# A hybrid token mixer with a routed MoE on one core: issue points of front work moved

## The chip, the cores and the metric

The kernel runs on one core of one Trainium2 chip. The metric is device microseconds of the whole program; lower is better. The times before are the median of three runs.

## The reference

One layer, 1024 tokens of width 1024, all in float32.

1. A conditioning vector gives six rows (shift, scale and gate, two times): `mod = silu(c) @ w_mod + b_mod`, six blocks of 1024.
2. `h = rms_norm(x) * (1 + sc1) + sh1`, then one projection to 2576 columns, split into three mixers: gated linear attention (GLA: q, k, v, output gate, and a low-rank decay gate), RetNet retention (q, k with rotation, v, gate), and an S5 state-space layer (16 groups of 16 channels with a complex state of 64, a scan over time, GELU and a GLU).
3. Attention layers work in chunks of 64 tokens: scores inside a chunk, a state from chunk to chunk; each head's output is normalised and multiplied by its gate. The three results are concatenated and sent through an output projection: `x = x + g1 * mixed @ w_out`.
4. `h2 = rms_norm(x) * (1 + sc2) + sh2`; a router picks 4 of 32 experts for each token; each expert is an up projection, a clamped SwiGLU and a down projection; the gated sum is added, then a final norm.

## The kernel before

Each float32 weight is used as two f16 parts (high and low); a product is three matmuls. `split` makes the parts: the high part on ACT (L182), the low part on DVE (L183). A projection of one tile (`proj_group`, lines 729 to 733) is 24 matmuls of 128 x 384, with a call `mid()` in the middle at which other work is issued.

The 1024 tokens are eight tiles of 128. The front (up to 578 us) has three stages, and the MoE follows. In the front the order in the program is the order of each engine's queue: an engine takes its instructions one after the other, and an instruction that waits holds up all behind it on its engine. PSUM tiles come in four tags: `j` (2 banks), `g` (3), `s` (2), `o` (1).

**First pass (to about 105 us).** The modulation rows, the norm of each tile (`n1_sum`, `n1_norm`, `n1_turn`, `n1_scale`), `n1_split` (the transposed tile as high and low f16; the low part by a subtraction at L673 on POOL, or on DVE), then `n1_proj`: S5's input and the decay gate (L187 belongs to it, through `mm3`). Behind the last tile come the first tile's projections q/k, g and v, with steps of `prep` in between.

**GLA loop (L1230 and on, to about 324 us).** Round h has `gla_decay(h)` (exponentials on ACT, L1070 to L1072), `gla_qk(h)` (projection and five DVE products), `gla_scores(h - 1)`, `gla_gate(h)`, `gla_out(h - 1)`, `gla_turn(h)`, `gla_v(h)` and `gla_norm(h - 1)`. In between, `filler(n)` takes the next n steps of a generator: S5 first, then the second weight set. S5 has four rounds b of `s5_products` (INJ on DVE at L900 to L902; its transposes to injT, L907; GE on POOL, L911 to L913; KS, L919; eight DMAs; cosine and sine tables) and `s5_scan` (L936, L942 with L945 and L946, the scan, L957, L967 and L970), then `s5_gate` with the GELU and four GLU pieces (L1013 to L1022). `weights2` splits the retention weights (`split_next`, which also issues the next weight load) and computes modulation blocks 2 and 3.

**Third pass (L1549 and on, to 578 us).** Round i starts with three loads on SP (`load_res(i)`: the tile's x, tile `x3` with two buffers; `load_hT(i + 2)`; `load_rope(i + 2)`), then `ret_qk(i + 1)` with the rotation on DVE, `ret_scores(i)`, `out_a(i - 1)` (output projection, first part), `out_turn(i - 2, 0)`, `ret_out(i)` (state, attention, head statistics), `ret_gate(i + 1)`, `out_turn(i - 2, 1)` (copy on DVE, L617), `ret_norm(i)`, `out_b(i - 1)`, `out_route(i - 2)` (router, top 4; L186 to L188 and L1475 on), `ret_v(i + 1)`, `out_place(i - 2)` (places in the expert lists, L1501, and four scatter DMAs on POOL), `ret_turn(i + 1)` (four transposes, L1323), `ret_end(i)` (transposes of the head output, L864), `out_rms(i - 1)` and `out_norm(i - 1)` (the norm of the next layer: L1445 on DVE, L1446 and L1449 on POOL). The old x tile is the scratch of that norm, so its buffer comes free when the subtraction at L1449 is done. The calls `f()` take steps of `weights3`:

```python
for k in OUT_ORDER: split_next(wO...); yield        # eight splits
split(rw16...); yield
for ac in mod_block(4): yield                       # row load, then 8 products L378
...; for sl, p in mod_rows(ac): ... a2 ...; yield   # L385 on PE, L1530 on DVE
ready.add("a2")
for ac in mod_block(5): yield                       # the same for block 5
... g2c (L1538 on PE)
```

`mod_block(b)` clears `ac` on POOL (L374), loads the bias row on SP (L375), and yields; then each step is one DVE product (L378) and one more weight load (`load_next`, L223). `ac` has one buffer. `out_norm(0)` reads a2, so a loop takes steps until `"a2"` is in `ready`.

**MoE (L1722 and on).** Blocks of rows are gathered by the id table that the scatters of `out_place` wrote, and run through the experts; weights stream in by SP.

Of the kernel before, what the change touches and what calls it, by code (L numbers as in the profile page):

```python
# [11 lines left out]
F32 = mybir.dt.float32  # L12
# [9 lines left out]
NT = T // 128  # L22
# [6 lines left out]
C_GQ, C_GK, C_GV, C_GG, C_GA = 0, 192, 384, 768, 1152  # L29
# [94 lines left out]
def build(ctx, tc, A, out, dbg=None):  # L124
# [269 lines left out]
    LR, LI = UC, US  # L394
# [271 lines left out]
    def n1_split(i, eng=G, parts=1):  # L666
        if i < NT:
            hd = hds.pop(i)
            hT = ht1[i] = p1.tile([128, 2, 8, 128], F16, name="hTa", bufs=3)
            for q in range(parts):  # L670
                ks = slice(q * 8 // parts, (q + 1) * 8 // parts)
                S.copy(hT[:, 0, ks], hd[:, ks])
                eng.tensor_tensor(hT[:, 1, ks], hd[:, ks], hT[:, 0, ks], op=SUB)  # L673
# [103 lines left out]
    rest = load_rest()  # L777
    for i in range(NT):
        def ahead():
            n1_split(i + 1)  # L780
            n1_norm(i + 2)
            if i == 0:
                n1_sum(3)

        n1_proj(i, ahead)
        n1_decay(i - 1)
        n1_turn(i + 2)
        n1_scale(i + 2)
        n1_store(i + 1)
        if i in (0, 1, 2):  # L790
            load_next()
        fill(rest)
        if i in (3, 4):
            load_hT(i - 3)
        if i == 5:
            s5_turned()
        if i == 6:
            s5_bias()
        fill(prep, 4)
        split_next(wA[:, 0, i, :], wA[:, 1, i, :], GLA_COLS)  # L800
        n1_sum(i + 4)
# [2 lines left out]
    gpj = {"qk": proj_group(hTs[0], wA, C_GQ, C_GV, mid)}  # L804
    mid()
    gpj["g"] = proj_group(hTs[0], wA, C_GG, C_GA, mid)
    mid()
    gpj["v"] = proj_group(hTs[0], wA, C_GV, C_GG, mid, "s")
    for _ in prep:
        pass  # L810
    dump("suT", suT.rearrange("p m l n -> p (m l n)"))
# [75 lines left out]
    def s5_products(b, B):  # L887
        gs = slice(4 * b, 4 * b + 4)
        GE = B["GE"] = s5w.tile([128, 4, 9, SH], F32, name="GE")
        tg = s5w.tile([128, 4, 8, SH], F32, name="tg", bufs=1)  # L890
        INJ = s5w.tile([128, 4, SL, SH], F32, name="INJ", bufs=1)

        def ch(x, q, n):
            return x[:, 4 * b + q, None, :].to_broadcast([128, n, SH])

        def pw(x, q, n):
            return x[:, 4 * b + q, 0:n, None].to_broadcast([128, n, SH])

        for q in range(4):
            V.tensor_tensor(INJ[:, q], ch(bb, q, 8), pw(LR, q, 8), op=MULT)  # L900
            V.tensor_tensor(tg[:, q], ch(bp, q, 8), pw(LI, q, 8), op=MULT)
        V.tensor_tensor(INJ, INJ, tg, op=SUB)  # L902
        yield
        injT = B["injT"] = s5w.tile([128, 4, 128], F32, name="injT", bufs=1)
        p = pst(tag="s")
        for q in range(4):
            PE.transpose(p[:, q * 128:(q + 1) * 128], INJ[:, q].rearrange("p l h -> p (l h)"), ident)  # L907
        S.copy(injT.rearrange("p g x -> p (g x)"), p)
        tg = s5w.tile([128, 4, 9, SH], F32, name="tG", bufs=1)
        for q in range(4):  # L910
            G.tensor_tensor(GE[:, q], ch(CA, q, 9), pw(LR, q, 9), op=MULT)  # L911
            G.tensor_tensor(tg[:, q], ch(CB, q, 9), pw(LI, q, 9), op=MULT)
        G.tensor_tensor(GE, GE, tg, op=ADD)  # L913
        yield
        yield
        KS = s5w.tile([16, 4, 128], F32, name="KS", bufs=1)
        p = pst(tag="s")
        for q in range(4):
            PE.matmul(p[0:16, q * 128:(q + 1) * 128], bb[:, 4 * b + q, :],  # L919
                      GE[:, q, 0:8, :].rearrange("p l h -> p (l h)"),  # L920
                      start=q == 0, stop=q == 3, skip_group_check=True)
        S.copy(KS.rearrange("p g x -> p (g x)"), p[0:16, :])
        V.tensor_tensor(KS[:, :, 0:16], KS[:, :, 0:16], drow[:, gs, :], op=ADD)
        yield
        TP = TPs[b % 2]
        for l in range(SL):
            r = SL - 1 - l
            SY.dma_start(TP[16 * r:16 * r + 16, :, 16 * l:128], KS[:, :, 0:128 - 16 * l])
        yield from s5_tables(b, B)
# [162 lines left out]
    def gla_v(i, mid):  # L1092
        p = gpj.pop("v") if i == 0 else proj_group(hTs[i], wA, C_GV, C_GG, mid)
        v = L[i]["v"] = p2.tile([128, 384], F32, name="v")
        S.activation(v, p, AF.Copy, scale=UN)
# [132 lines left out]
    for i in range(-1, NT):  # L1228
        h = i + 1
        n = 2 if left["s5"] else 1  # L1230
        f1 = lambda: filler(1)
        f2 = lambda: filler(n)
        if h < NT:
            gla_decay(h)
            gla_qk(h, f2)
        else:
            rpj["d"] = proj_group(hTs["r0"], pBc["wB"], 0, 384, f2)
            ret_rope(0, rpj["d"], pBc["rope"])
        f2()
        if i > 0:  # L1240
            gla_end(i - 1)
        if i >= 0:
            gla_scores(i)
        f1()
        if h < NT:
            gla_gate(h, f2)
        else:
            rpj["g"] = proj_group(hTs["r0"], pBc["wB"], 768, 1152, f2)
        f2()
        if i >= 0:  # L1250
            gla_out(i)
        f1()
        if h < NT:
            gla_turn(h)
            gla_v(h, f2)
            load_hT(h + 2)
            if h + 2 == NT:
                load_hT(0, "r0")
            elif h + 1 == NT:
                load_hT(1, "r1")  # L1260
        else:
            rpj["v"] = proj_group(hTs["r0"], pBc["wB"], 384, 768, f2, "s")
        if i >= 0:
            gla_norm(i)
        f2()
        f1()
    for _ in left["w2"]:
        pass
    gla_end(NT - 1)
# [42 lines left out]
    def ret_gate(i, mid, p=None):  # L1312
        R[i]["gate"] = silu_gate(p3, proj_group(hTs[i], wB, 768, 1152, mid) if p is None else p, rnw)
# [234 lines left out]
    for i in range(NT):  # L1548
        h, b, t = i + 1, i - 1, i - 2  # L1549
        hd, ob, ot, last = h < NT, 0 <= b, 0 <= t, i == NT - 1  # L1550
        f = lambda: fill(w3)
        load_res(i)
        load_hT(h + 1)
        load_rope(h + 1)
        if hd:
            ret_qk(h, f)
        f()
        ret_scores(i)
        f()
        if last:  # L1560
            break
        if ob:
            out_a(b)
        if ot:
            out_turn(t, 0)
        f()
        ret_out(i)
        f()
        ret_gate(h, f)
        f()  # L1570
        if ot:
            out_turn(t, 1)
        ret_norm(i)
        if ob:
            out_b(b)
        if ot:
            out_route(t)
        ret_v(h, f)
        if ot:
            out_place(t)  # L1580
        ret_turn(h)
        ret_end(i)
        while b == 0 and "a2" not in ready:
            f()
        if ob:
            out_rms(b)
            out_norm(b, int(h == NT - 1))
        f()
# [522 lines left out]
```

## Time and profile before

| | us |
|---|---|
| median of three runs | 1885.22 (1882.71 to 1889.75) |
| profiled execution | 1887.09 |
| its span | 1885.4 |
| PE busy | 1743.0 (92%) |
| DVE busy | 1582.1 (84%) |
| ACT busy | 1232.8 (65%) |
| POOL busy | 574.7 (30%) |

Columns of the table by stage name engines in the order PE, PEld (weight loads), DVE, ACT, POOL. PE is TensorE, DVE VectorE, ACT ScalarE, POOL GpSimd, and SP issues most DMAs. A row of a timeline has the start, the length of time (us), engine, line, operation, output and inputs by the program's names with their shapes, and in brackets how long the engine was idle before it and what ended that. Rows with xN hold N instructions in a row. PEclk is the granted TensorE clock, 1.00 being 2.4 GHz and 0.50 being 1.2 GHz.

### The profile page before, as it was taken

The page shows a single profiled execution, that of the slowest core. Times are in us where ns is not written, and L with a number is a line of the kernel's source. Part 1 is how long each engine was busy: PE and PEld are TensorE (multiplying, and loading weights), DVE is VectorE, ACT ScalarE, POOL GpSimd, SP SyncE. Part 2 cuts the span into 40 slices and gives each one's busy share as a digit, 9 for nine tenths or more (in the row PEclk, how much of TensorE's full clock was granted, in tenths as well). Part 3 has the DMA queues.
Part 4 walks back from the last instruction along what each step waited for, and adds up shares of the span by engine and source line. Part 5 has one row for each costly group of instructions (what it writes and reads, how often), then busy time and mean ns, then how long its engine had stood idle before and what let it go on. Part 6 is the DMA issues. An engine that isn't in the chain of part 4 may idle for free.

```text
span 1885.4 us, 57406 instructions
## 1 busy us (share of the span) xinstructions
PE 1743.0 (92%) x23174; PEld 1553.2 (82%) x23174; DVE 1582.1 (84%) x2430; ACT 1232.8 (65%) x1714; POOL 574.7 (30%) x532
## 2 busy tenths in 40 slices
PE   6889989899983999999999999999999999999984
PEld 3756666556643899999999999999999999999983
DVE  7858677765565988888899999999999999999985
ACT  2722333212224777877888888888888888888874
POOL 3833110143524222231231312213323343323214
PEclk9989999999995999999999999999999999999997
DMA  8841246632217999999999999999999999999985
GB/s 295 285 110 41 57 141 195 226 115 97 74 68 267 332 314 325 348 328 337 336 345 362 369 364 369 363 368 366 363 372 375 354 367 359 365 367 359 368 299 214
DMA packets 182268, 535.34 MB, mean 284 GB/s; under 512 B 30078, under 2 KB 40248, under 8 KB 181964
## 3 DMA queue, kind: packets, MB, share of 16 engines
q1 hardware_dynamic: 167548, 490.92, 71.7%
q0 software_dynamic: 14160, 39.64, 8.5%
q8 instruction: 183, 3.00, 0.6%
q10 hardware_dynamic: 288, 1.05, 0.1%
q14 instruction: 89, 0.73, 0.1%
HBM read 490.77 MB, written 40.17 MB: 282 GB/s over the span
## 4 chain that ended last, share of the span: by engine, by line
PE 60%; ACT 2%; issue 2%; DMA 2%; DVE 2%; POOL 1%; SPq 0%; DVEq 0%; ACTq 0%; POOLq 0%
PE ac L1789 19%; PE ac L1791 18%; PE ac L1790 18%; PE tp L1876 3%; PE tp L1744 2%; ACT wh L1890 2%; DMA wf<-in_w_up_dram 1%; DVE wl L1891 1%; POOL fs L1952 0%; DMA wf<-in_w_down_dram 0%; DVE el L1828 0%; DMA idtab<-pairs,dest 0%; ACT yT L1862 0%; POOL fs L1953 0%; DVE eg L1806 0%
## 5 line engine op out<-in xcount | busy, mean ns | idle before, releaser
L1891 DVE SCALAR_TENSOR_TENSOR wl<-wf,wh 128x1024 f16<-128x1024 f32 x768 | 943.5, 1269 | 112.7 <-ACT wh L1890 102.6
L1890 ACT ACTIVATE wh<-wf 128x1024 f16<-128x1024 f32 x768 | 772.3, 1054 | 26.7 <-DMA wf<-in_w_up_dram 9.2
L1791 PE MATMUL ac<-xT,wl 128*128 128x108 f16 (+27 forms) x4096 | 766.9, 225 | 3.9 <-DVE wl L1891 3.8
L1789 PE MATMUL ac<-xT,wh 128*128 128x108 f16 (+27 forms) x4096 | 767.3, 226 | 0.5 <-ACT xT L1745 0.3
L1790 PE MATMUL ac<-xT,wh 128*128 128x108 f16 (+27 forms) x4096 | 766.8, 225 | 0.7 <-ACT xT L1745 0.7
L1791 PEld LDWEIGHTS <-wl 128*128 128x128 f16 x6144 | 600.9, 98 | 8.9 <-DVE wl L1891 7.1
L1790 PEld LDWEIGHTS <-wh 128*128 128x128 f16 x6144 | 602.1, 98 | 4.3 <-issue 2.8
L1789 PEld LDWEIGHTS <-wh 128*128 128x128 f16 x6144 | 601.4, 98 | 1.8
L1789 PE MATMUL ac<-aT,wh 128*128 128x108 f16 (+27 forms) x2048 | 378.2, 225 | 1.9 <-DVE eg L1806 1.9
L1791 PE MATMUL ac<-aT,wl 128*128 128x108 f16 (+27 forms) x2048 | 378.2, 225 | 1.1 <-DVE wl L1891 0.9
L1790 PE MATMUL ac<-aT,wh 128*128 128x108 f16 (+27 forms) x2048 | 378.1, 224 | 0.6 <-DVE aT L1842 0.6
L1879 POOL DMA_INDIRECT acc_d<-yr,ids x51 | 133.9, 2626 | 572.6 <-ACT yr L1877 392.2
L1812 POOL TENSOR_TENSOR eg<-eg,es 128x432 f32<-128x432 f32 (+28 forms) x74 | 101.6, 1373 | 296.7 <-ACT es L1811 294.9
L1839 ACT ACTIVATE aT<-el 128x432 f16<-128x432 f32 (+28 forms) x74 | 45.2, 611 | 94.3 <-DVE el L1832 90.9
L1862 ACT ACTIVATE yT<-ac,BALL,g2s 128x136 f32<-128x136 f32 (+27 forms) x256 | 97.7, 472 | 8.7 <-PE ac L1791 8.6
L1811 ACT ACTIVATE es<-eg 128x432 f32<-128x432 f32 (+28 forms) x74 | 44.8, 605 | 77.9 <-DVE eg L1806 76.1
L1732 POOL DMA_INDIRECT xr<-h2s,ids x52 | 85.6, 1646 | 31.4 <-issue 10.2
L1745 ACT COPY xT<-tp 128x1024 f16<-128x1024 f16 (+27 forms) x104 | 75.8, 729 | 25.8 <-PE tp L1744 25.7
L1744 PE MATMUL tp<-id,xr 128*128 128x128 f16 (+27 forms) x832 | 53.4, 201 | 25.8 <-DMA wf<-in_w_up_dram 23.5
L1828 DVE TENSOR_SCALAR el<-ac,BALL 128x136 f32<-128x136 f32 (+27 forms) x256 | 75.9, 355 | 0.0
L1806 DVE TENSOR_SCALAR eg<-ac,BALL 128x136 f32<-128x136 f32 (+27 forms) x256 | 74.8, 354 | 0.5 <-PE ac L1791 0.5
L1876 PE MATMUL tp<-C,yT 128*128 128x128 f32 (+6 forms) x408 | 66.2, 280 | 8.7 <-ACT yT L1862 8.5
(496 smaller groups left out, 2423.9 us busy)
## 6 DMA issues: line engine op xcount, KB each, us to landing
wf<-in_w_up_dram SPq DMA_DIRECT2D x512, 512.0 KB
wf<-in_w_down_dram SPq DMA_DIRECT2D x256, 512.0 KB
wst<-in_w_mod_dram SPq DMA_DIRECT2D x40, 512.0 KB
wst<-in_w_in_dram SPq DMA_DIRECT2D x16, 576.0 KB
x<-in_x_dram SPq DMA_DIRECT2D x16, 512.0 KB
hTb<-hT_d SPq DMA_DIRECT2D x16, 512.0 KB
wA<-in_w_mod_dram SPq DMA_DIRECT2D x8, 512.0 KB
hT_d<-hTa SPq DMA_DIRECT2D x8, 512.0 KB
```

Source lines behind the costliest of these rows:

```text
L1732: G.indirect_dma_start(out=x, out_offset=None, in_=h2s[:, :], in_offset=bass.IndirectOffsetOnAxis(ap=self.ids[j][:, 0:1], axis=0))
L1744: PE.transpose(p[:, k, :], self.xr[j][0:c, kk_ * 128:(kk_ + 1) * 128], id16[0:c, 0:c])
L1789: PE.matmul(dst, h[:, ms], xh, start=k == 0 and m % x.per == 0, stop=False, skip_group_check=True)
L1790: PE.matmul(dst, h[:, ms], xl, start=False, stop=False, skip_group_check=True)
L1791: PE.matmul(dst, l[:, ms], xh, start=False, stop=k == 7, skip_group_check=True)
L1812: G.tensor_tensor(g, g, s, op=MULT)
L1828: V.tensor_scalar(t[i][:, q, :], self.loc(i + q), x.bias(8 + m), 8.0 * SS, op0=ADD, op1=MIN)
L1862: S.activation(x.yT[:, m, 0:x.n], self.loc(i), AF.Identity, scale=g2s[:, m:m + 1], bias=x.bias(16 + m))
L1876: PE.transpose(p[0:c, m * 128:(m + 1) * 128], x.yT[:, q * 4 + m, r0:r0 + c], ident)
L1879: G.indirect_dma_start(out=acc_d[:, :], out_offset=bass.IndirectOffsetOnAxis(ap=x.ids[j][:, 0:1], axis=0), in_=y, in_offset=None, compute_ ...
L1890: S.activation(h, w, AF.Copy, scale=SW)
L1891: V.scalar_tensor_tensor(l, w, SW, h, op0=MULT, op1=SUB)
```

## The change

Eight places are issued at another point. No work is added or taken out; the first part cuts one copy and one subtraction into two.

1. `n1_split` of the last tile: the low part in two halves on DVE, not on POOL.
2. The v projection of tile 0, with the step of `prep` ahead of it, leaves the first pass; the projection is issued in round 0 of the GLA loop behind `gla_qk(0)`, and that round begins with one filler step (INJ, and now GE, of S5's first round).
3. In `s5_products`, GE's nine POOL operations are issued with INJ, a step earlier than before.
4. In the GLA loop, the filler step at the end of a round is taken between `gla_turn(h)` and `gla_v(h)`.
5. In the third pass, `out_rms(0)` and `out_norm(0)`, with the loop that waits for a2, go from the end of round 1 to round 2, behind `ret_qk(3)`.
6. In round 0, `ret_gate(1)` goes ahead of `ret_out(0)`.
7. `ret_turn(h)` goes ahead of `out_place(t)`.
8. `ret_end(0)` goes from the end of round 0 to round 1, behind `ret_qk(2)`.

```diff
@@ -777,7 +777,7 @@
     rest = load_rest()
     for i in range(NT):
         def ahead():
-            n1_split(i + 1)
+            n1_split(i + 1, *((V, 2) if i + 2 == NT else ()))
             n1_norm(i + 2)
             if i == 0:
                 n1_sum(3)
@@ -804,8 +804,6 @@
     gpj = {"qk": proj_group(hTs[0], wA, C_GQ, C_GV, mid)}
     mid()
     gpj["g"] = proj_group(hTs[0], wA, C_GG, C_GA, mid)
-    mid()
-    gpj["v"] = proj_group(hTs[0], wA, C_GV, C_GG, mid, "s")
     for _ in prep:
         pass
     dump("suT", suT.rearrange("p m l n -> p (m l n)"))
@@ -900,17 +898,17 @@
             V.tensor_tensor(INJ[:, q], ch(bb, q, 8), pw(LR, q, 8), op=MULT)
             V.tensor_tensor(tg[:, q], ch(bp, q, 8), pw(LI, q, 8), op=MULT)
         V.tensor_tensor(INJ, INJ, tg, op=SUB)
+        tg = s5w.tile([128, 4, 9, SH], F32, name="tG", bufs=1)
+        for q in range(4):
+            G.tensor_tensor(GE[:, q], ch(CA, q, 9), pw(LR, q, 9), op=MULT)
+            G.tensor_tensor(tg[:, q], ch(CB, q, 9), pw(LI, q, 9), op=MULT)
+        G.tensor_tensor(GE, GE, tg, op=ADD)
         yield
         injT = B["injT"] = s5w.tile([128, 4, 128], F32, name="injT", bufs=1)
         p = pst(tag="s")
         for q in range(4):
             PE.transpose(p[:, q * 128:(q + 1) * 128], INJ[:, q].rearrange("p l h -> p (l h)"), ident)
         S.copy(injT.rearrange("p g x -> p (g x)"), p)
-        tg = s5w.tile([128, 4, 9, SH], F32, name="tG", bufs=1)
-        for q in range(4):
-            G.tensor_tensor(GE[:, q], ch(CA, q, 9), pw(LR, q, 9), op=MULT)
-            G.tensor_tensor(tg[:, q], ch(CB, q, 9), pw(LI, q, 9), op=MULT)
-        G.tensor_tensor(GE, GE, tg, op=ADD)
         yield
         yield
         KS = s5w.tile([16, 4, 128], F32, name="KS", bufs=1)
@@ -1231,8 +1229,12 @@
         f1 = lambda: filler(1)
         f2 = lambda: filler(n)
         if h < NT:
+            if h == 0:
+                filler(1)
             gla_decay(h)
             gla_qk(h, f2)
+            if h == 0:
+                gpj["v"] = proj_group(hTs[0], wA, C_GV, C_GG, lambda: None, "s")
         else:
             rpj["d"] = proj_group(hTs["r0"], pBc["wB"], 0, 384, f2)
             ret_rope(0, rpj["d"], pBc["rope"])
@@ -1252,6 +1254,7 @@
         f1()
         if h < NT:
             gla_turn(h)
+            f1()
             gla_v(h, f2)
             load_hT(h + 2)
             if h + 2 == NT:
@@ -1263,7 +1266,8 @@
         if i >= 0:
             gla_norm(i)
         f2()
-        f1()
+        if h >= NT:
+            f1()
     for _ in left["w2"]:
         pass
     gla_end(NT - 1)
@@ -1555,6 +1559,13 @@
         if hd:
             ret_qk(h, f)
         f()
+        if i == 1:
+            ret_end(0)
+        if i == 2:
+            while "a2" not in ready:
+                f()
+            out_rms(0)
+            out_norm(0)
         ret_scores(i)
         f()
         if last:
@@ -1564,9 +1575,13 @@
         if ot:
             out_turn(t, 0)
         f()
-        ret_out(i)
-        f()
-        ret_gate(h, f)
+        if i == 0:
+            ret_gate(h, f)
+            ret_out(i)
+        else:
+            ret_out(i)
+            f()
+            ret_gate(h, f)
         f()
         if ot:
             out_turn(t, 1)
@@ -1576,13 +1591,12 @@
         if ot:
             out_route(t)
         ret_v(h, f)
+        ret_turn(h)
         if ot:
             out_place(t)
-        ret_turn(h)
-        ret_end(i)
-        while b == 0 and "a2" not in ready:
-            f()
-        if ob:
+        if i > 0:
+            ret_end(i)
+        if b > 0:
             out_rms(b)
             out_norm(b, int(h == NT - 1))
         f()
```

## Rows read from the trace of the kernel before

**Rows 1.** Table by stage: start:end, length, busy (count) per engine, PEclk, DMA share, GB/s

```profile
100.00:324.00 224.00, 204.75 (x1233) 138.46 (x1231) 163.75 (x368) 63.11 (x114) 50.98 (x73) 0.95 0.36 103
324.00:578.00 254.00, 223.43 (x1518) 136.69 (x1516) 166.18 (x438) 66.39 (x120) 87.37 (x128) 0.94 0.34 115
578.00:1885.00 1307.00, 1240.17 (x19728) 1222.83 (x19728) 1173.17 (x1446) 1052.54 (x1399) 380.31 (x281) 0.98 0.98 347
```

**Rows 2.** The chain of waits, at the start of the MoE

```profile
578.25 4.52 DMA idtab<-pairs,dest
```

**Rows 3.** PE's waits, 90 to 420 us: us in total, times, longest

```profile
PE ps_s L907 <- issue: 4.1, 1, 4.1
PE ps_o L385 <- DVE ac L378: 3.2, 2, 2.5
PE ps_s L919 <- POOL GE L913: 3.2, 2, 1.7
PE ps_g L1122 <- ACT ex L1071: 3.1, 1, 3.1
PE ps_g L1063 <- DVE q2T L1114: 2.7, 1, 2.7
PE ps_o L1501 <- DVE m L1491: 2.4, 1, 2.4
PE ps_g L1133 <- DVE scR L1337: 2.4, 1, 2.4
PE ps_g L864 <- ACT hh L182: 2.4, 2, 2.1
PE ps_g L187 <- POOL hTa L673: 2.2, 1, 2.2
...
PE ps_o L186 <- DVE hT L617: 0.9, 1, 0.9
```

**Rows 4.** The same table for short stretches (engines PE, PEld, DVE, ACT, POOL)

```profile
121.00:133.00 12.00, 10.96 (x36) 7.50 (x37) 9.82 (x22) 4.73 (x9) 2.14 (x3) 0.50 0.20 56
245.00:250.00 5.00, 4.09 (x17) 2.69 (x18) 3.19 (x7) 1.78 (x5) 3.46 (x7) 0.66 0.13 39
331.00:338.00 7.00, 5.11 (x34) 3.49 (x35) 6.81 (x19) 1.59 (x2) 2.04 (x5) 1.00 1.00 399
375.00:383.00 8.00, 7.65 (x31) 3.88 (x32) 4.28 (x6) 0.41 (x2) 2.97 (x4) 0.79 0.57 197
383.00:401.00 18.00, 18.00 (x112) 10.80 (x111) 16.61 (x29) 2.55 (x3) 7.04 (x8) 1.00 0.64 216
```

**Rows 5.** Timelines of POOL and DVE, the low halves of tiles 7 and 0

```profile
91.73 3.26 POOL L673 TENSOR_TENSOR hTa<-hd,hTa 128x1024 f16<-128x1024 f32 x1 [1.16 <-ACT hTa L672]
...
42.28 3.00 DVE L673 TENSOR_TENSOR hTa<-hd,hTa 128x512 f16<-128x512 f32 x2 [1.09 <-ACT hTa L672]
```

**Rows 6.** Timeline of DVE, round 0 of the GLA loop

```profile
115.62 0.36 DVE L1082 SCALAR_TENSOR_TENSOR k<-ps_j,en 128x192 f32<-128x192 f32 x1 [6.88 <-POOL GE L913]
...
130.91 1.76 DVE L902 TENSOR_TENSOR INJ<-INJ,tg 128x512 f32<-128x512 f32 x1
```

**Rows 7.** Timeline of ACT, round 0 of both loops

```profile
121.23 1.28 ACT L824 ACT_TABLE_LOAD   x1
...
336.22 1.06 ACT L182 ACTIVATE wO<-wst 128x1024 f16<-128x1024 f32 x1 [5.86 <-DMA wst<-in_w_out_dram]
```

**Rows 8.** Timeline of SP, start of round 2 of the third pass

```profile
388.36 0.33 SPq L1416 DMA_DIRECT2D x<-in_x_dram  x1
```

**Rows 9.** Timeline of POOL, the norm of tile 0

```profile
386.20 2.13 POOL L1449 TENSOR_TENSOR hl<-x,hl 128x1024 f16<-128x1024 f32 x1 [1.16 <-ACT hl L1447]
```

**Rows 10.** Timeline of DVE, block 3's first product and tile 1's norm

```profile
303.96 1.28 DVE L378 SCALAR_TENSOR_TENSOR ac<-wst,cond,ac 128x1024 f32<-128x1024 f32 x1 [2.26 <-DMA ac<-in_b_mod_dram]
...
416.58 1.28 DVE L1445 SCALAR_TENSOR_TENSOR x<-x,rs,a 128x1024 f32<-128x1024 f32 x1 [6.20 <-POOL rs L161]
```

**Rows 11.** Timeline of PE, round 3 of the third pass

```profile
442.66 0.18 PE L1501 MATMUL ps_o<-m,strict 128*128 128x32 f16 x1 [0.69 <-DVE m L1491]
```

## The prediction

> **What bounds the kernel now.** I began with the table by stage. From 578 us on, in the MoE, PE is busy 1240 of 1307 us and the DMA share is 0.98; in the two stages ahead PE is busy 205 of 224 and 223 of 254 us, DVE 164 and 166, and the DMA share is 0.36 and 0.34 [rows 1]. Then the chain of waits: the MoE begins behind the landing of an id scatter that the front's last tile issues [rows 2]. So the change touches the front alone, and a microsecond less on what limits the front, PE, is one less of the total. The third view was what PE waited for between 90 and 420 us: ten rows hold 27 us of gaps [rows 3]. The fourth was the granted clock around such gaps: 0.50 from 121 to 133 us, 0.66 at 245 to 250, 0.79 at 375 to 383, but 1.00 at 331 to 338, where a gap of 2.4 lies [rows 4]. Most long gaps cost twice, as a gap and as matmuls at the lower of the two levels: in PE's 10.96 busy us at 0.50 about 5.5 us are lost, in 4.09 at 0.66 about 1.4, in 7.65 at 0.79 about 1.6 (busy time times one less the clock).
>
> **A, the last tile's low halves (L780).** PE waited 2.2 us for this subtraction on POOL [rows 3], which takes 3.26 us; the first tile's, in two halves on DVE, took 3.00 [rows 5]. The first half is enough for PE to start, and it waits for half the copy only. I take +2.0 (a gain); bounds 0 (DVE held by the next scale) to 3.8 (the gap, and clock as at 375).
>
> **B, the first tile's value projection and INJ0.** The longest gap of the front is 4.1 us, ahead of L907 [rows 3]: INJ0's nine operations stood behind the five q/k products, which waited for ex, while DVE had idled 6.88 us [rows 6]. Five products of 0.36 are 1.8, so INJ0's nine take the other 2.3. With filler(1) first they run in the idle time, and the 24 matmuls of the value projection, moved behind decay(0), cover ex. This gap goes. But the steps behind it need ACT's tanh with its table load of 1.28 us [rows 7], then DVE: from 121 to 133 us it was busy 9.82 of 12 us in 22 operations [rows 4] (silu, the cosine and sine products, gla_turn's copies, INJ1, whose last operation took 1.76 us [rows 6]). PE now comes to the load of INJ0 some 4 us earlier, so the tanh can end about 2.5 earlier, near 120.2; 9 us of DVE's work behind it put INJ1's end near 129. Before, decay(1) and half of a projection stood ahead of the transposes of INJ1; now these stand ahead of decay(1). PE, ready at about 122.5, waits until 129, and the clock has no reason to rise. I take 0; bounds -3 (INJ1 later by POOL's GE1 beside it) to +9 (the gap, and 5 of the 5.5 us of clock).
>
> **C, GE one step earlier.** PE waited 3.2 us in two places for GE's last operation on POOL [rows 3]. POOL has 51 of 224 us of work in this stage [rows 1] and now gets the nine operations before L946. +2.5; bounds -1 (L946 late on the scan's chain) to 3.2.
>
> **D, a filler between gla_turn and gla_v.** The S5 steps and the weight splits come a filler or two earlier against PE's work. The gap of 3.1 for ex [rows 3] comes from ACT, where the GLU's rounds stand ahead of the exponentials; a round earlier, most of it goes, with the 1.4 of clock: +3.5. The 2.7 for q2T [rows 3] comes from DVE with the splits; the same operations only change order, so I count +0.5 of it, nearer to nothing than to the whole. Bounds -1 (a split ahead of another waited operation) to +7.2 (3.1, 1.4, 2.7). +4.
>
> **F and H, a projection ahead of the first retention output, ret_end(0) later.** F fills the 2.4 for scR, where no clock was lost [rows 3, 4]. It also puts the state and norm of tile 0 behind one more weight split, and those were at the pace of the loads there: ACT waited 5.86 us for one at 336.22 [rows 7], so tile 0's hh comes later. H moves ret_end(0), which waited up to 2.1 for it [rows 3], behind a projection; with fewer gaps ahead, PE still comes early. +1.5; bounds -2 (both gaps stay at the new places, with half clock) to +6 (both go, and 1.6 of clock).
>
> **E, the norm of tile 0 behind ret_qk(3).** It takes away the 2.5 us for ac at L385 [rows 3] and 1.6 of clock, as the projection and DVE's rope now lie in it. Against it stands SP's queue. Before, the bias row of modulation block 5 was issued ahead of load_res(2). That load needs the third buffer of x, so it waits for tile 0's subtraction on POOL: this ended at 388.33, the load went out at 388.36 [rows 8, 9]. Now load_res(2) is issued at the start of i = 2, and behind it stand hT, rope, one weight block and only then the row. The norm comes a projection and a rope later in DVE's order but without the 2.5 gap, so the subtraction again ends near 387.6. The row then goes out near 389.6 behind 1.5 MB (three loads of 512 KB), 3.8 us at the 399 GB/s of the busiest window [rows 4], and lands near 394.5. DVE stands ahead of block 5's first product from about 382.7 until then: 12 us, with the states of tile 2, its statistics, silu(3) and the low half's copy (L617) behind it. From 383 to 401 us PE was busy 18.00 of 18 us and DVE 16.61 [rows 4], so DVE can take in little of the 12. PE comes to the routing product, which needs that copy, near 398 and waits until 405; before, it waited 0.9 [rows 3]. The placement follows at 412 instead of 409.2. Block 5's last product stands behind tile 1's norm (L1445), which waits for POOL's scatters, 6.20 us before [rows 10], so L1538, now between scores(3) and out_a(2), waits for it, about 5 us. That makes -10 at the states of tile 3, 2.8 and 5 and half clock behind each, less the 4.1 gained: -6.5 with a little taken in. Bounds -17 (all 12 and the 5 reach PE) to +6.5 (the row in time: 2.5, 1.6, and the 2.4 for L1501).
>
> DMA order has a rule that speaks against this part. The Trainium skill, "DMA: Bandwidth & Descriptors", section "Queues, rings and completion order", says that on each DMA engine the descriptors of one issuer's queue are taken in ring order. By it the row cannot pass the 1.5 MB; a row like it held DVE for 2.26 us with nothing ahead of it [rows 10], so without the rule it would land near 392, and E would be about -4. No row here shows a small load passing a large one.
>
> **G, ret_turn ahead of out_place.** Four waits at L1501, the first at 442 and one in each later round, are 0.69 us [rows 11], and ret_turn's four transposes, 0.6 us, fill them. +2.5; bounds 0 (ACT's copies of the turn late) to 2.8.
>
> **Sum.** 2 + 0 + 2.5 + 4 + 1.5 - 6.5 + 2.5 = +6.0 us. The profiled execution took 1887.1 (span 1885.4 and 1.7 around it): 1881.1. It lies 1.9 over the median of the three, 1885.2, and from that the same sum gives 1879.2. I take 1880.
>
> **Rivals.** First, the row is not late: E is +4.1 to +6.5 and the sum 17 to 19, so 1867 to 1870. For it: a DMA share of 0.34 in this stage [rows 1]. Against it: the load at 388.36 that followed the subtraction at once [rows 8, 9].
>
> Second, the slower side, E's place at its worst: all 12 us of DVE's stop and L1538's 5 reach PE, 10.5 more than I count, sum -4.5: 1890 to 1892; with the row at 398 another 3.5, 1893 to 1895. It decides at the landing of the row: from about 391 on (DVE can take in some 8 us of stop before PE's 18 us of work run out), each microsecond goes to PE. Against it: PE needs nothing from DVE in most of these 18 us.
>
> Third, the waits only move. A, C, D, F and H show PE's next gap, as B does, because DVE and ACT have the same work in the same order among themselves. The sum is near 0, 1885 to 1887. For it: DVE 16.61 of 18 and 9.82 of 12 us [rows 4]; against it: DVE busy only 164 of 224 [rows 1].
>
> **Chances.** The forecast 0.42 (its own range 1874 to 1886), the first rival 0.28, the second 0.13, the third 0.17. About 0.5%, 9.4 us, is what a measurement of this kernel can tell from no change. Faster by more than that: the first rival and 0.08 of the forecast, 0.36; slower: the worse part of the second, 0.08; within: 0.56. The range, 1866 to 1892, goes from the first rival with a little of B's bound to the second.
>
> **What would show it.** A: no wait at L187. B: no gap at L907, but 5 us or more at the transposes of INJ1. C: no wait for L913. D: under 1 us for ex. E: DVE stopped ahead of block 5's first product until the bias row lands, PE waiting at L186 for the copy of L617, then at L1538. G: no 0.69 at L1501. If PE waits under 2 us at that L186, the forecast is too slow by some 10 us; if the gaps of A, C and D are back elsewhere at their old sizes, it is too fast by 8.

## The result, and the profile after

The changed kernel takes 1904.7 us (median of five runs, 1896.0 to 1906.8) against 1885.2 before; the ratio is 1.0086 with a 95% interval of 1.0067 to 1.0104, so it is slower by some 13 to 20 us. The profiled execution took 1898.5 us, 11.4 more than that of before, and is one of the two shorter ones; the other three took some 7 us more, at a mean granted clock of 0.959 (0.964 and 0.968 in the two), and none of them was traced. So the traces, which are compared with each other, show the lower end of that range. Line numbers of after are larger by up to 4 in the third pass (L1538 is L1542, L1416 is L1420) and smaller by 2 in parts of the GLA loop; the transposes of INJ, L907, are L910.

The table by stage of after (columns as in [rows 1]) shows the MoE much as before, and in the third pass less work done by 578 us:

```profile
100.00:324.00 224.00, 201.96 (x1198) 135.42 (x1196) 160.32 (x368) 61.69 (x111) 50.20 (x73) 0.95 0.36 102
324.00:578.00 254.00, 222.49 (x1475) 136.49 (x1474) 154.88 (x392) 60.28 (x112) 78.81 (x109) 0.94 0.33 109
578.00:1896.00 1318.00, 1242.44 (x19778) 1223.94 (x19777) 1184.55 (x1493) 1058.03 (x1407) 381.44 (x300) 0.97 0.97 346
```

DVE did 154.88 us of work in the third pass' stretch, 166.18 before [rows 1]: its work was not through by 578. The chain of waits has the last scatter that the MoE stands behind at 593.44, 15.2 us later than [rows 2]:

```profile
593.44 6.68 DMA idtab<-pairs,dest
```

PE's waits from 90 to 420 us, and from 420 to 580, answer to [rows 3]:

```profile
PE ps_o L186 <- DVE hT L617: 9.6, 1, 9.6
PE ps_s L910 <- DVE INJ L900: 8.3, 3, 4.0
PE ps_g L862 <- ACT hh L182: 3.2, 1, 3.2
PE ps_o L385 <- DVE ac L378: 2.7, 2, 1.4
...
PE ps_s L955 <- DVE xs L950: 2.0, 1, 2.0
PE ps_g L1120 <- ACT ex L1069: 1.4, 2, 1.0
...
PE ps_o L1542 <- issue: 8.7, 1, 8.7
```

Of the waits that the parts were to take away, those for GE and scR and that of L907 in S5's first round are gone, and ex fell from 3.1 to 1.4; the one for hh stays (3.2), and L385 still has 2.7. New ones of the same kind stand in the later S5 rounds (L910, the line of L907, waits 8.3 us for INJ in three of them; xs 2.0), and two of 9.6 and 8.7 us in rounds 2 and 3 of the third pass. The clock follows them: in the stretches of the two, 397 to 413 and 420 to 433 us, it is 0.70 and 0.65.

```profile
397.00:413.00 16.00, 6.40 (x45) 3.19 (x44) 14.57 (x31) 0.52 (x1) 3.77 (x6) 0.70 0.53 176
420.00:433.00 13.00, 4.26 (x23) 4.01 (x23) 9.02 (x11) 1.04 (x1) 8.35 (x9) 0.65 0.04 8
```

What made the first is in the timelines of POOL, SP and DVE (one after the other), the answer to [rows 8 to 10]. The norm's subtraction ends at 388.98, load_res(2) goes out at 389.01, the bias row of block 5 behind three loads and a weight block at 390.81, and DVE, idle 13.54 us, starts block 5 at 397.44. Later the norm of tile 1 waits 6.21 us for POOL behind the scatters, and only then comes the pair of products that L1542 needs. The pair takes 4.56 us beside POOL's addition, which takes 3.31; without the other engine beside them a pair took 2.60 (397.44) and the addition 2.36 (383.34):

```profile
383.34 2.36 POOL L1450 TENSOR_TENSOR x<-x,sh 128x1024 f32<-128x1024 f32 x1 [1.40 <-DVE x L1449]
386.85 2.13 POOL L1453 TENSOR_TENSOR hl<-x,hl 128x1024 f16<-128x1024 f32 x1 [1.15 <-ACT hl L1451]
...
424.90 3.31 POOL L1450 TENSOR_TENSOR x<-x,sh 128x1024 f32<-128x1024 f32 x1 [1.40 <-DVE x L1449]
...
389.01 0.33 SPq L1420 DMA_DIRECT2D x<-in_x_dram  x1
...
390.81 0.39 SPq L375 DMA_DIRECT2D ac<-in_b_mod_dram  x1
...
397.44 2.60 DVE L378 SCALAR_TENSOR_TENSOR ac<-wst,cond,ac 128x1024 f32<-128x1024 f32 x2 [13.54 <-DMA ac<-in_b_mod_dram]
...
423.54 1.28 DVE L1449 SCALAR_TENSOR_TENSOR x<-x,rs,a 128x1024 f32<-128x1024 f32 x1 [6.21 <-POOL rs L161]
424.74 4.56 DVE L378 SCALAR_TENSOR_TENSOR ac<-wst,cond,ac 128x1024 f32<-128x1024 f32 x2
```

### The profile page after: what moved, and what is told of

It reads as the page before. It is cut to its first block, busy times and chain, and to the rows that moved or that the text cites. A ratio compares the mean times of both kernels' runs of the same rounds, so it can differ in the third digit from the quotient of the medians.

```text
span 1896.8 us, 57405 instructions
## 1 busy us (share of the span) xinstructions
PE 1743.0 (92%) x23174; PEld 1551.6 (82%) x23174; DVE 1579.9 (83%) x2432; ACT 1232.0 (65%) x1715; POOL 563.2 (30%) x531
## 3 DMA queue, kind: packets, MB, share of 16 engines
q10 hardware_dynamic: 288, 1.05, 0.1%
## 4 chain that ended last, share of the span: by engine, by line
PE 60%; ACT 2%; DMA 2%; issue 2%; DVE 1%; POOL 1%; SPq 0%; POOLq 0%; DVEq 0%; ACTq 0%
PE ac L1803 19%; PE ac L1804 18%; PE ac L1805 18%; PE tp L1890 2%; PE tp L1758 2%; ACT wh L1904 2%; DMA wf<-in_w_up_dram 1%; DVE wl L1905 1%; DMA ids<-idtab 0%; POOL fs L1966 0%; ACT yT L1876 0%; DMA idtab<-pairs,dest 0%; DMA wf<-in_w_down_dram 0%; POOL fs L1967 0%; DVE eg L1820 0%
## 5 line engine op out<-in xcount | busy, mean ns | idle before, releaser
L1893 POOL DMA_INDIRECT acc_d<-yr,ids x51 | 126.3, 2476 | 574.1 <-ACT yr L1891 391.3
## 6 DMA issues: line engine op xcount, KB each, us to landing
wA<-in_w_mod_dram SPq DMA_DIRECT2D x8, 512.0 KB, 10.4
```

The source lines that it names most:

```text
L1893: G.indirect_dma_start(out=acc_d[:, :], out_offset=bass.IndirectOffsetOnAxis(ap=x.ids[j][:, 0:1], axis=0), in_=y, in_offset=None, compute_ ...
```

## The experiments

Each kernel's time is its ratio to the kernel before, run on the same chip in the same rounds. The table goes by the traces: how much later (+) or earlier PE starts the same matmuls than before, at the last attention of the GLA loop (314.9 us before; counted from tile 7's decay-gate product, 87.92 before, since the loads of the first 85 us shift a trace by up to 2.8 us), then what the third pass adds up to the attention of its round 3 (428.2 before), then the first matmul of the MoE (599.3, uncounted shift included).

```
kernel                 GLA end   third pass adds   MoE      ratio [95%]
changed                 +0.9       +14.4          +14.2   1.0086 [1.0067, 1.0104]
undo_norm0              +1.6        +2.8           +4.1   1.0011 [0.9995, 1.0026]
norm0_alone             +1.7       +12.6          +15.8   1.0055 [1.0037, 1.0072]
x2_behind_norm          +1.0        +7.4           +8.4   1.0030 [1.0008, 1.0053]
x2_behind_g2c_later     +3.1        -4.3 (+1.3)    +6.4   1.0000 [0.9983, 1.0017]
low7_alone              -3.7        +2.3           +0.5   1.0003 [0.9986, 1.0019]
v0_alone               +13.5        +3.5          +16.5   1.0089 [1.0063, 1.0115]
step_only              +15.4        +1.1          +15.9   1.0061 [1.0042, 1.0080]
v0_no_filler            -1.9        +3.6           +3.6   0.9989 [0.9976, 1.0002]
ge_alone                +2.9        +2.4           +4.2   1.0021 [1.0010, 1.0032]
filler_alone            -0.7        +0.4           +1.2   0.9990 [0.9977, 1.0004]
gate_end_alone           0.0        +5.6           +4.7   1.0012 [0.9999, 1.0026]
norm_before_place       -2.1        +6.7           +7.0   1.0041 [1.0027, 1.0056]
e_mended                +0.2        -8.0 (-6.2)    -6.7   0.9969 [0.9955, 0.9983]
best1                   -4.7        -7.6           -10.0   0.9958 [0.9944, 0.9972]
best2                   -5.0        -7.6 (-5.8)    -10.5   0.9950 [0.9934, 0.9966]
```

In brackets: a round later, where it differs. Four rows have the first pass and the GLA loop of before and show -2.1 to +1.7 there, so about 2 us is what one trace against one other can't tell. Six rows have the third pass of before and add 0.4 to 3.6 there, 2.2 on average: the profile of before was a good one at that place, with 2.1 us of wait for hh where low7_alone has 4.2. The parts of the third pass are read against +2.2, with the same uncertainty.

**E undone.**

```diff
-        if i == 2:
-            while "a2" not in ready: f()
-            out_rms(0); out_norm(0)
+        (the loop and the norm of tile 0 at the end of round 1, as before)
```

> The changed kernel with part E undone: the norm of tile 0 stands at the end of round 1 again, all other parts stay. Theory 1 (the placement of that norm alone makes the change slower, the other parts come to about nothing): PE's wait at L186 falls from 9.6 us to under 2, the one of 8.7 us at L1542 goes, the 2.5 us at L385 come back, and the time is within 4 us of before, 1882 to 1889. Rival (the loss is spread, since the front's steps in front of the third pass crowd DVE): still 6 us or more slower than before, 1891 or more.

Measured: 1889.6 us, ratio 1.0011. L186 waits 0.2 us, L1542 0.2, and L385 has 5.0 in one wait. Theory 1 holds, but for the size at L385: without E the other parts come to about nothing (-1 to +5 us by the interval).

**E alone.** The edit is part 5 of the change.

> The kernel before with part E alone: the norm of tile 0 issued in round 2 behind the projection of tile 3. Theory 1: both waits of the changed kernel appear, 8 to 10 us at L186 and 6 to 9 at L1538, less about 3 us for the wait at L385 that goes; the MoE begins 13 to 16 us later than before and the time is 1897 to 1902. Rival (E loses only because the other parts brought PE there earlier): under 6 us slower, below 1891.

Measured: 1897.8 us, 1.0055. PE's waits between 320 and 540 us:

```profile
PE ps_o L1538 <- issue: 8.6, 1, 8.6
PE ps_o L186 <- DVE hT L617: 6.7, 1, 6.7
...
```

Theory 1 holds; only the wait at L186 is shorter than it said. The time is 10.8 us above before. The third pass adds 12.6, some 10 more than the six kernels with the old one.

**One load moved.**

```diff
-        load_res(i)
+        if i != 2:
+            load_res(i)
...
             out_norm(0)
+            load_res(2)
```

> The changed kernel with one load moved: load_res(2) is issued behind out_norm(0) instead of at the start of round 2; the norm stays where the change put it. Theory 1 (the bias row of block 5 waits on SP behind load_res(2), which waits for the buffer that this norm frees): the row goes out near 381 instead of 390.8 and DVE's stop of 13.5 us ahead of block 5's first product falls to under 4; the 9.6 us at L186 fall to under 2. The wait at L1542 (8.7 us) stays, since it hangs on the norm of tile 1 behind the scatters: 5 to 10 us. Time 7 to 10 us less than the changed kernel. Rival (the norm stands too late for DVE and POOL, whatever SP does): L186 still waits 6 us or more and the time is within 3 us of the changed kernel.

Measured: 1893.3 us, 1.0030, by the two ratios some 10 us less than the changed kernel (5 to 16 by the intervals). The row is issued at 384.24 and DVE waits 1.12 us for it (timelines of SP and DVE):

```profile
384.24 0.25 SPq L375 DMA_DIRECT2D ac<-in_b_mod_dram  x1
...
388.21 1.75 DVE L378 SCALAR_TENSOR_TENSOR ac<-wst,cond,ac 128x1024 f32<-128x1024 f32 x1 [1.12 <-DMA ac<-in_b_mod_dram]
```

The wait at L186 is gone and the one at L1542 is 9.1 us. One load, issued ahead of the norm whose buffer it takes, was nearly the whole of DVE's stop: 13.54 us have become 1.12.

**And block 5's turn two steps later.** The edit adds two empty steps ahead of the matmuls of L1542.

```diff
+        for _ in range(2):
+            yield
         p = pst(tag="o")
```

> As the one before, and L1542 (the turn of block 5's sums) two steps of the generator later, behind the state products of round 3. Theory 1 (L1542 stood at a point where its last product could not be done): the wait there falls from 8.7 us to under 2, and the time is another 5 to 9 us less than with the load moved alone, so 1880 to 1888, not slower than before. Rival (the wait only names the order of DVE, and PE waits as long at the next product that needs DVE): within 3 us of the kernel with the load moved alone.

Measured: 1887.8 us, ratio 1.0000 [0.9983, 1.0017]. The wait at L1542 is gone and the step from the kernel above is 5.5 us, as theory 1 has it, though the intervals of the two ratios overlap. But the trace keeps less than it should: by the traces' own times PE is 3.8 us ahead of before at the scores of round 3 and 5.5 behind a round later. Part of this is L1542's own matmuls (3.4 us), which now lie between the two points and lay ahead of both before. The rest is a wait for tile 1's norm, the one that waits for POOL's scatters of tile 0, and a clock of 0.51 from 426 to 436.5 us, in which PE was busy 10.13 us:

```profile
425.33 0.62 PE L616 MATMUL ps_o<-id,hl 128*128 128x128 f16 x8 [2.56 <-ACT hl L1451]
```

**A alone.** The edit is part 1.

> The kernel before with part A alone (the low half of tile 7 on DVE). The changed kernel reached the first projection behind the first pass 3.0 us earlier. Theory (A gives these 3 us, gap and clock, and they last): the wait of 2.2 us at L187 falls under 1, the GLA loop and the MoE begin 2 to 4 us earlier, time 1 to 4 us less than before. Rival (a chain of waits further on, of the third pass, sets the pace and eats it): the GLA loop begins 3 us earlier, the rounds of the third pass under 1 us earlier.

Measured: 1885.5 us, 1.0003 [0.9986, 1.0019]. L187 waits 0.8 us for DVE, and the GLA loop ends 3.7 us earlier, gap and clock. In the third pass the wait for hh is 4.2 instead of 2.1, behind ACT's split of w_out, which waits 6.59 us for its load. But the third pass adds 2.3 us, as it does on average in the six kernels that have it as before, so it isn't shown that A's microseconds are lost there. The interval goes from 2.6 us less to 3.6 more: the theory holds for the GLA loop, and whether the gain reaches the total stays open.

**B alone, its step alone, its projection alone.** The edits: part 2; only its first two lines (filler(1) at the start of round 0); only the projection.

> The kernel before with part B alone (v of tile 0 into the GLA loop, one filler step ahead of it). Theory (the gap at L907 goes and comes back at the transposes of INJ1 or ahead of it): no wait at L907, decay(0) about 4 us earlier, decay(1) at most 1 us earlier than before, the clock of the stretch between them still near half; time within 3 us of before. Rival (B works, and the loss in the changed kernel is due to the filler of part D): decay(1) and all behind it 4 to 8 us earlier, no wait over 1 us there.

> The kernel before with one filler step more at the start of round 0 of the GLA loop, and nothing else moved (the value projection of tile 0 stays in the first pass). Theory (one step ahead is what cost part B alone its 15 us): waits of 4 us or more at the transposes of INJ1 and for GE in the later rounds, end of the GLA loop 8 us or more later against its start, time 6 to 16 us more than before. Rival (it takes the step and the moved projection together): end of the loop within 4 us, time within 4 us of before.

> The kernel before with the value projection of tile 0 moved into round 0 of the GLA loop as in part B, but without the filler step at the start of that round. Theory (what made part B alone 15 us slower is the one step by which all S5 work then runs ahead of DVE and POOL, not the projection's place): the waits of 8.7 us at the transposes of INJ1 and 5.6 us for GE are not there, the wait at L907 is under 2 us since the projection covers ex, decay(1) 1 to 4 us earlier; time 0 to 4 us less than before. Rival (the projection's place makes the loss): decay(1) 2 us or more later than before and time 6 us or more above it.

Measured: 1901.7 us (1.0089), 1898.1 (1.0061) and 1885.1 (0.9989). For B alone both forecasts of the time were wrong. The theory's first half held: the gap of L907 in S5's first round went and came back as one of 8.7 us at the same transposes of the second (L905 in that kernel), and decay(1) is 1.1 us later than before. But then the GLA loop lost 12 us more. The third run clears the projection, with a wait of 1.8 instead of 4.1 at L907; the second shows the same loss from the step alone. Its waits from 100 to 324 us:

```profile
PE ps_s L919 <- POOL GE L913: 7.2, 2, 5.6
PE ps_s L907 <- DVE INJ L902: 5.5, 1, 5.5
...
```

and POOL's timeline says why GE is late: the head statistics' power, which waits for DVE, stands ahead of GE's nine operations. It did so before, at 177.28 with GE from 181.53; here it comes at 182.24 and GE from 184.46, while PE asks for GE a step earlier.

```profile
182.24 1.02 POOL L843 TENSOR_TENSOR rst<-rst,mhalf 128x4 f32<-128x4 f32 x1 [13.15 <-DVE rst L842]
```

A generator that runs one step ahead shifts every S5 step behind it, against all engines, for four rounds; the mean clock of the stage fell from 0.95 to 0.90. In the changed kernel, where C has GE a step earlier, no wait for GE is left, and A to D together come to +0.9, where the four alone add up to +12: such parts don't add. No run shows which of C and D undoes B's loss.

**C alone.** The edit is part 3.

> The kernel before with part C alone (GE issued a step earlier). Theory: the two waits for L913 (3.2 us in all) go and nothing takes their place; decay(4) 2 to 3.5 us earlier, time 1 to 4 us less than before. Rival (POOL's nine operations beside DVE slow DVE's, and L946 behind them holds up the scan): a wait for the scan or for INJ of 1 us or more appears, decay(4) under 1 us earlier.

Measured: 1891.2 us, 1.0021 [1.0010, 1.0032], slower. No wait for GE is left, but L907 has 6.1 instead of 4.1 us in round 0 and 2.8 in round 2. The rival holds, by its first half. DVE's timeline of round 2 in the kernel before, then in this one:

```profile
154.55 0.28 DVE L900 TENSOR_TENSOR INJ<-bb,UC 128x128 f32<-128x128 f32 x1
...
155.07 0.69 DVE L902 TENSOR_TENSOR INJ<-INJ,tg 128x512 f32<-128x512 f32 x1
```

```profile
159.07 0.51 DVE L900 TENSOR_TENSOR INJ<-bb,UC 128x128 f32<-128x128 f32 x1
...
159.82 1.77 DVE L902 TENSOR_TENSOR INJ<-INJ,tg 128x512 f32<-128x512 f32 x1
```

In the same time POOL did GE, from 155.56 on, its last operation 1.53 us from 159.51. INJ took 5.1 us (156.45 to 161.59) instead of 2.4.

**D alone.** The edit is part 4.

> The kernel before with part D alone (the filler between gla_turn and gla_v). Theory 1 (the S5 steps now come ahead of the DVE work that feeds them, so PE stands before the transposes of INJ): waits of 3 to 5 us at L907 in rounds 1 and 2, the 3.1 us for ex goes; at the end of the GLA loop 0 to 4 us later than before, time 0 to 4 us more. Rival (it was B and C that made INJ late): no wait over 1.5 us at L907 behind round 0, the loop ends 3 to 5 us earlier.

Measured: 1885.6 us, 0.9990 [0.9977, 1.0004]. The wait for ex is 2.0 instead of 3.1; L907 waits 1.1 and 0.6 in rounds 2 and 3. Neither forecast: the waits are a third of theory 1's and the loop ends 0.7 earlier, not 3 to 5. The rival's first half is right, for behind round 0 no wait at L907 is over 1.5 us. D moves small waits and comes to nothing that can be measured.

**F and H alone.** The edits are parts 6 and 8.

> The kernel before with parts F and H alone (gate(1) ahead of the first retention output, ret_end(0) in round 1). Theory (the two waits go, the loads of w_out then set when tile 0's head output is ready): no wait for scR behind 330, the wait for hh moves to round 1 and is 2 to 4 us; scores of round 1 0 to 3 us earlier against the last transposes of the GLA loop, time within 3 us of before. Rival (both waits go for good): 4 to 6 us earlier from round 1 on, time 4 to 6 us less.

Measured: 1889.1 us, 1.0012 [0.9999, 1.0026]. No wait for scR, 3.4 for hh, and a longer one at L385: 4.6 us instead of 2.5. I put this down to part 6, which drops one f() in round 0, so that every step of weights3 comes one place later; that wasn't run by itself. The theory's two waits are as told; the loss at L385 was in neither.

**The placement behind the norm.**

```diff
-        if ot:
-            out_place(t)
         ret_turn(h)
...
             out_norm(b, int(h == NT - 1))
+        if ot:
+            out_place(t)
```

> The kernel before with the placement of tile t issued behind the norm of tile t + 1 in each round of the third pass, so that POOL does the norm's small operations and its add ahead of the four scatters. Theory (rounds 2 to 6 are paced by a chain, placement, four scatters on POOL, norm, turn, routing, placement, of 28.4 us, and not by PE with 27.7; this is why part G gained nothing): the waits of 0.69 us at L1501 go, a round takes 27.6 to 27.9 us instead of 28.37, the wait of 6.2 us of DVE for the norm goes, and the MoE begins 3 to 6 us earlier; time 2 to 6 us less. Rival (PE or DVE sets the round): a round stays at 28.3 us or more with waits of the same sum at other places, time within 1.5 us of before or above it.

Measured: 1894.0 us, 1.0041, slower. L1538 waits 5.1 us, since it needs the one bank of tag o that the placement now holds until DVE is past the norm, and the rounds take 29 to 30 us, not 27.7. The head statistics' power now waits for the scatters on POOL, DVE for it, and PE for the routing (POOL's, DVE's and PE's timelines):

```profile
467.51 1.61 POOL L1347 TENSOR_SCALAR Sr<-Sr 64x96 f32<-64x96 f32 x3 [3.14 <-DMA idtab<-pairs,dest]
469.21 1.04 POOL L843 TENSOR_TENSOR rst<-rst,mhalf 128x4 f32<-128x4 f32 x1
...
470.29 0.95 DVE L851 TENSOR_SCALAR yh<-ps_g,mv,rst 128x96 f32<-128x96 f32 x3 [1.92 <-POOL rst L843]
...
477.53 0.18 PE L1501 MATMUL ps_o<-m,strict 128*128 128x32 f16 x1 [1.92 <-DVE m L1491]
```

My theory was wrong about the cure: at the new place, too, something waits behind POOL's 5 us of scatters. That a chain through them sets the round this run doesn't show, since it got longer; rows on this follow under G below.

**E mended, and two combinations.** e_mended: E alone, with load_res(2) behind the norm, block 5's turn two steps later, and in round 2 alone the placement behind the norm. best1: that with A, D, F and H, and the placement behind the norm in every round. best2: the same with it in round 2 only.

```diff
-        if ot:
+        if ot and i != 2:
             out_place(t)
...
             out_norm(b, int(h == NT - 1))
+        if i == 2:
+            out_place(0)
```

> The kernel before with part E alone and its three obstacles taken away: load_res(2) behind the norm of tile 0, the turn of block 5's sums two steps later, and the placement of tile 0 behind the norm of tile 1 (in that round only). Theory (E's own gain is the gap at L385 with its clock and what POOL's scatters cost the norm of tile 1; it lasts once nothing waits behind load_res(2), block 5 and the scatters): no wait over 2 us at L186, L1538 or the turn of tile 1 in rounds 2 and 3, the rounds from 3 on 5 to 9 us earlier against the end of the GLA loop, time 3 to 8 us less than before. Rival (E gains nothing by itself and the gain of best1 comes from its other parts): within 2 us of before.

> A version put together from the parts that gained or lost nothing: A, D, F and H, E with load_res(2) behind the norm and the turn of block 5's sums two steps later, and the placement behind the norm in every round; B, C and G left out. Theory (the front's time is then no longer held by the placement chain, so that E's gain of 5 to 8 us lasts): the MoE begins 6 to 12 us earlier, time 5 to 11 us less than before. Rival (the loads of w_out at the start of the third pass and DVE hold it anyway): within 3 us of norm_before_place.

> As best1, but with the placement behind the norm in round 2 only; the later rounds as in the kernel before. In best1 the rounds 3 to 6 were 29.0 to 29.9 us instead of 28.4, with waits of 0.9 to 2.1 us at L1501, since the head statistics' power on POOL then stood behind the four scatters. Theory (the order of rounds 3 to 6 cost these 3 us): rounds of 28.4 us, the MoE 2 to 4 us earlier than in best1, time 1874 to 1879. Rival (the chain of the placement takes them back): within 1.5 us of best1.

Measured: 1882.2 us (0.9969), 1879.4 (0.9958) and 1876.7 (0.9950 [0.9934, 0.9966]). With its obstacles away E comes to a gain, 6 us in the time. The placement behind the norm in round 2 alone and the later turn of block 5 weren't run without E, so a share of the 6 may be theirs. In the traces of best1 and best2 the GLA loop ends 5 us earlier as well, near what A and D gave there alone (-3.7 and -0.7); in the times best2 and e_mended can't be told apart. best2 beats both kernels, by about 9 us and 26 us. From round 4 on its rounds are at 28.4 us, 10.6 us ahead of before by the traces' own times; its time agrees with both its theory and, within the intervals, best1, so the order of the later rounds is not settled by time. Its waits from 320 to 540 us have neither of the two long ones:

```profile
PE ps_o L1503 <- DVE m L1493: 4.2, 5, 1.4
PE ps_g L864 <- ACT hh L182: 3.4, 1, 3.4
PE ps_o L616 <- ACT hl L1449: 1.8, 1, 1.8
PE ps_o L385 <- DVE ac L378: 1.6, 1, 1.6
...
```

## Why the prediction was wrong

The sign was wrong: +6 us of gain against a loss of 14 us in the traces at the start of the MoE, 11 at their end, and 13 to 20 in the times. The step that failed is the sum: E's loss, whose mechanism was right, was put too small, and the gains of A to D and of G were put at 11 us together where the runs show about -1.

- **E, -6.5 in the sum; -10.4 alone (12.6 less the 2.2), -11.6 in the changed kernel (14.4 against 2.8 without it).** Place and mechanism were as told, and the second rival's: the row behind load_res(2), L186 waiting for L617's copy, then L1542. Each size was short. The row landed 6.6 us after its issue, not 4.9: four loads stood ahead of it, 1.7 MB with the rope's 192 KB, where the working has three. DVE stood 13.5 us, not 12; L186 waited 9.6, not 7; L1542 8.7, not 5, and 2 of that are the product that POOL's addition held up, which no term has. Both stretches ran at 0.65 to 0.70 of the clock, in PE's 10.7 busy us a loss of 3.4, where -10 less the 2.8 and 5 leaves some 2 for it. The last step of the working is off as well: -10 and the 4.1 gained make -5.9, not -6.5.

  A row of before, from SP's timeline, gives what such a row needs with nothing ahead of it: it was issued at 302.34 and DVE began at 303.96 [rows 10], 1.6 us later.

```profile
302.34 0.25 SPq L375 DMA_DIRECT2D ac<-in_b_mod_dram  x1
```

  The prediction's rule of the Trainium skill ("DMA: Bandwidth & Descriptors", section "Queues, rings and completion order") has the descriptors of one issuer's queue taken in ring order on each DMA engine. By that rule, the trace agrees: 6.6 us behind 1.7 MB, 1.6 alone.
- **A to D, +8.5 in the sum, -0.9 measured.** Alone, A was +3.7 for my +2, in the GLA loop. D was +0.7 for +4. C was -2.9 for +2.5: I asked only what POOL's work had in front of it and not who works beside it. The Trainium skill, "SBUF — State Buffer", section "SBUF: two separate sides", says that DVE operations with two SBUF inputs and GpSimd's share a port that one of them holds alone for a whole operation. By that rule the trace agrees (0.28 to 0.51, 0.69 to 1.77 us), most plainly beside tile 1's norm, where product, addition and product end one after the other (426.0, 428.2 and 429.3). A row of this kind stood in [rows 6], where I took the 1.76 for a cost and not for a warning. B was -13.5 alone, where my bound was -3: I followed the step through one round and not through four.
- **F and H, +1.5 in the sum, about -3 alone** (+5.6 less 2.2), 2.1 of it at L385. The size is uncertain: with a like wait of 5.0 at L385, F, G and H in undo_norm0 come to -0.6 (+2.8 less 2.2).
- **G, +2.5 in the sum, about 0.** It was not run alone; the trace of after shows it. The 0.69 us of [rows 11] became 0.26 there and 0.31 at the next turn:

```profile
457.82 0.18 PE L1505 MATMUL ps_o<-m,strict 128*128 128x32 f16 x1 [0.26 <-DVE m L1495]
...
469.94 0.45 PE L616 MATMUL ps_o<-id,hl 128*128 128x128 f16 x5 [0.31 <-ACT hl L1451]
```

and from one L1505 to the next it is 28.4 us, as before. PE is busy for 27.8 of them. By these rows, what holds the period is the way from the placement through scatters and norm to the turn's first transposes (L616), which start 12.12 us behind L1505 here, as they did behind L1501 before (454.78), and from there 16.3 us through PE, routing and DVE to the next placement. Before, PE came to these transposes just as ACT's copy was done (453.67 and 1.05 are 454.72); with ret_turn's 0.6 us moved ahead, PE comes earlier and waits 0.31 there. The rows of before, of ACT and of PE:

```profile
453.67 1.05 ACT L1447 CAST hl<-x 128x1024 f16<-128x1024 f32 x1 [7.39 <-POOL x L1446]
...
454.78 0.61 PE L616 MATMUL ps_o<-id,hl 128*128 128x128 f16 x8
```

"A microsecond less on what limits the front, PE, is one less of the total" was the sentence all gains rested on, and it holds only where PE is that limit.

The third rival (the waits only move) described A to D well, though A's own gap did not come back in the GLA loop; I gave it 0.17.

## What to carry to other kernels

Before work that frees a buffer is moved, list what is queued on the load engine behind the load that takes this buffer: here one 512 KB load held back a 4 KB row, and that row DVE. A gap in a busy engine is worth its length only if that engine sets the round; compare the round's period with the engine's work in it, and look for the loop of waits that closes over the round. When steps come from a generator, taking one more or one fewer at one place moves every later step, so such an edit is to be followed to the generator's end.

## What the runs showed of the hardware that was not expected

DVE's operations with two inputs in SBUF slow down by a factor of 1.8 to 2.6 beside POOL's (0.28 to 0.51 us, 0.69 to 1.77 in ge_alone; 1.28 to 3.24 for the second product beside tile 1's norm in the changed kernel). POOL's small ones lost little there (0.42 to 0.47 us, one 0.87), its large addition took 3.31 instead of 2.36. A 4 KB load issued behind 1.7 MB on the same queue takes 6.6 us instead of 1.6 until DVE begins. In the two stretches of the changed kernel with waits of 9.6 and 8.7 us the clock was at 0.70 and 0.65.
